# One 512-column product for the hi weights in the last feed-forward, with the second block's divided at changing columns

## The chip, the cores and the metric

The kernel runs on one core of one Trainium2 chip. The metric is the device time of one execution in microseconds. Times are compared by the median of several runs; one execution is also recorded by the hardware profiler, and all durations below come from that one.

## What is computed

One inference step of a small two-layer transformer backbone for two groups of 128 tokens each: 128 context tokens and 128 latent tokens, model width 2048. Both groups use the same weights, so the kernel treats them as one operand with 256 token columns (NT = 256). Each layer has an attention mixer and a gated feed-forward with a three-wide convolution over the tokens:

```python
def conv_ffn(h, w_up, w_conv, b_conv, w_down):
    u = h @ w_up                                  # 2048 -> 2 * 5632
    up = jnp.pad(u, ((0, 0), (1, 1), (0, 0)))
    u = up[:, :-2] * w_conv[0] + up[:, 1:-1] * w_conv[1] + up[:, 2:] * w_conv[2] + b_conv
    gate, val = u[..., :D_FF], u[..., D_FF:]
    return (jax.nn.silu(gate) * val) @ w_down     # 5632 -> 2048
...
    h = rmsnorm(x, g_norm_ffn[l]) * (1 + sc2) + sh2
    x = x + gt2 * conv_ffn(h, w_ffn_up[l], w_ffn_conv[l], b_ffn_conv[l], w_ffn_down[l])
```

The factors sh, sc and gt come from a modulation product of the conditioning vector with w_ada. All data are float32.

## The kernel before, in words

**Products in three parts.** Activations lie with features on the partitions and the 256 tokens in the columns. To multiply at TensorE's reduced-precision float32 rate, each float32 operand is split into a hi part (rounded) and a lo part (the rest). A product of weights and operand is then hi·hi + hi·lo + lo·hi; lo·lo is dropped. The function `split` makes the parts: ScalarE casts the hi part (L238) and VectorE subtracts it for the lo part (L239). An operand row `hx[:, k]` holds 512 columns, the 256 of hi and behind them the 256 of lo (ROW = 512); the intermediate rows `g` of the feed-forward are laid out in the same way.

**One product.** `gemm` computes one output chunk of 128 features. It runs over the blocks of 128 input features: 16 in an up product, 22 in a down product. For each block it issues three matmuls of 256 columns into the same columns of one PSUM bank (tile acc, three banks in rotation): wh by x-hi, wh by x-lo, wl by x-hi. All matmuls are recorded under one helper's line, L105.

**Weights.** `Weights.chunk` hands out the blocks of a product. SP loads 1 MB tiles (raw, three buffers); the hi and lo parts are made 8 blocks at a time in tiles wh and wl with four buffers each, so that up to two up products can be made ahead of TensorE.

**The feed-forward** (`ffn`, called once for each layer) is done in two halves of the 5632 inner features. In each half, `up` makes 22 gate and 22 value products. After each, `conv` does the convolution: ScalarE scales and adds the bias (L1275), and VectorE adds the two neighbours (L1278, L1281), all three reading PSUM. SiLU, the product of gate and value (L1298) and their split into `g` follow. Then `down` makes 16 products of 22 blocks, and `residual` adds each to x with the gate factor, one VectorE instruction per token group (L775). The first products of a feed-forward are special: three are begun ahead, four more have a written order, and in five (list WIDER) the first matmul takes some columns more (32, 16, 8, 4 and 2) into unused columns of the bank.

**What sets the order.** A scheduler with a simulated timeline orders each engine's instructions; only some are kept in the written order. Between products, `pump` inserts part of the remaining modulation work; in the last feed-forward this is a product of a 2048-wide row on VectorE (L454, 2.3 us), 24 of them in all, spread at a rate of 0.7 per product until they are used up.

Of the kernel before, what the change touches and what calls it, by code (L numbers as in the profile page):

```python
# [13 lines left out]
ALU = mybir.AluOpType  # L14
# [3 lines left out]
P = 128  # L18
D = 2048
KD = D // P  # L20
T = 128
NT = 2 * T
ROW = 2 * NT
SHIFT = 320
NL = 2
# [30 lines left out]

EARLY = (2, 5, 8, 11, 13)
WIDER = (32, 16, 8, 4, 2)
SENT = (1, 3, 6, 9, 12, 14, 16)
FINE = 4  # L60

# [28 lines left out]
def step_kernel(ctx: ExitStack, tc: tile.TileContext, A: dict):  # L90
    nc = tc.nc
    dve, act, pool, sp = nc.vector, nc.scalar, nc.gpsimd, nc.sync
    kept = []

    def keep_order(i):
        if not any(i is j for j in kept):
            kept[:] = [i]
            tc.keep_in_program_order(i)
# [16 lines left out]
    pe = TensorE()  # L115
# [3 lines left out]
    tmp = ctx.enter_context(tc.tile_pool(name="tmp", bufs=2))  # L119
    small = ctx.enter_context(tc.tile_pool(name="small", bufs=4))  # L120
    pacc = ctx.enter_context(tc.tile_pool(name="pacc", bufs=3, space=PSUM))
# [5 lines left out]
    def banks(name):  # L127
        return tc.tile_pool(name=name, bufs=1, space=PSUM)
# [3 lines left out]
    def nm(s):  # L132
        uid[0] += 1
        return f"{s}_{uid[0]}"

    def T_(pl, shape, tag, dt=F32, bufs=None):
        kw = {} if bufs is None else {"bufs": bufs}
        return pl.tile(shape, dt, tag=tag, name=nm(tag), **kw)
# [50 lines left out]
    def stat_add(st, src, n, eng=pool):  # L189

        st["n"] += 1
        if st["n"] == 1:
            st["acc"] = T_(keep, [P, NT], "sqacc")
            act.activation(st["acc"], src, AF.Square)
            return
        sq = T_(tmp, [P, NT], "sq", bufs=2)
        act.activation(sq, src, AF.Square)  # L197
        if st["n"] == n:
            st["last"] = sq
        else:  # L200
            eng.tensor_tensor(out=st["acc"], in0=st["acc"], in1=sq, op=ALU.add)  # L201
# [35 lines left out]
    def split(out_hi, out_lo, src, pin=lambda i: i):  # L237
        pin(act.copy(out_hi, src))  # L238
        pin(dve.tensor_tensor(out=out_lo, in0=src, in1=out_hi.bitcast(F32), op=ALU.subtract))  # L239
# [84 lines left out]
    def gemm(blocks, xh, xl, n=NT, first=0, between=None, more=None):  # L324

        fixed = lambda i: keep_order(i) if between is not None else i
        ps = T_(pacc, [P, 512], "acc")
        last = len(blocks) - 1  # L330
        for i in range(last + 1):
            k = (i + first) % (last + 1)
            wh, wl = blocks[k]
            x0 = more(k) if more and i == 0 else xh(k)
            fixed(pe.matmul(ps[:, :x0.shape[-1]], wh, x0, start=(i == 0), stop=False))
            if callable(between):
                if i == (last + 1) // 2:
                    between()
            elif between and i in between:
                between[i]()  # L340
            fixed(pe.matmul(ps[:, :n], wh, xl(k), start=False, stop=False))
            fixed(pe.matmul(ps[:, :n], wl, xh(k), start=False, stop=(i == last)))
        return ps[:, :n]

    ada = {"i": 2, "t": 0, "due": 0.0, "pew": 1.0}
    feat = {"i": 0, "t": 0, "due": 0.0}
# [316 lines left out]
    def raw_tile(pl, tag):  # L665
        return home(pl, tag)[:, :KD * 2 * UW].rearrange("p (k n) -> p k n", k=KD)
# [105 lines left out]
    def residual(ps, l, which, c, st=None):  # L772
        for g in range(2):
            s = slice(g * T, (g + 1) * T)
            dve.scalar_tensor_tensor(out=x[:, c, s], in0=ps[:, s],  # L775
                                     scalar=mod[:, l, 3 * which + 2, c, g:g + 1],
                                     in1=x[:, c, s], op0=ALU.mult, op1=ALU.add)
        if st is not None:
            stat_add(st, x[:, c], KD)
# [467 lines left out]

    def ffn(hx, W, ready, turn, l, st):
        xh, xl = (lambda k: hx[:, k, :NT]), (lambda k: hx[:, k, NT:2 * NT])
        wider = list(WIDER)  # L1250

        def product():
            if ready:
                return ready.pop(0)
            if in_order:
                return gemm(W.chunk(), xh, xl, between=in_order.pop(0))
            if wider:
                n = NT + wider.pop(0)
                return gemm(W.chunk(), xh, xl, more=lambda k: hx[:, k, :n])
            return gemm(W.chunk(), xh, xl)  # L1260

        WD = Weights(A["w_down"][l], KQ, TB)
        cw = ada["cw"]
        with tc.tile_pool(name=f"ffn{l}", bufs=1) as fp, banks(f"pffn{l}") as pf:
            feat["home"], feat["pool"] = fp, pf
            feat["due"] = 0.0
            in_order = [{}, {}] + turn + [{}]
            T_(fp, [P, SHIFT // 4], "pad")

            def conv(m):  # L1270
                early = bool(ready)
                pin = keep_order if early else lambda i: i
                ps = product()
                y = T_(fp, [P, NT], "cv", bufs=3)
                pin(act.activation(y, ps, AF.Identity, scale=cw[:, 1, m:m + 1], bias=cw[:, 3, m:m + 1]))  # L1275
                y3 = y.rearrange("p (g t) -> p g t", g=2)
                p3 = ps.rearrange("p (g t) -> p g t", g=2)
                pin(dve.scalar_tensor_tensor(out=y3[:, :, 1:], in0=p3[:, :, :T - 1],  # L1278
                                             scalar=cw[:, 0, m:m + 1], in1=y3[:, :, 1:],
                                             op0=ALU.mult, op1=ALU.add))  # L1280
                pin(dve.scalar_tensor_tensor(out=y3[:, :, :T - 1], in0=p3[:, :, 1:],  # L1281
                                             scalar=cw[:, 2, m:m + 1], in1=y3[:, :, :T - 1],
                                             op0=ALU.mult, op1=ALU.add))
                if early and ready:
                    W.ahead(pin)
                return y

            def up(q):
                gs = []
                for i in range(q * KQ, (q + 1) * KQ):  # L1290
                    rate = 0 if i < LATE else FRATE["up"]
                    fine[0] = False
                    gate = conv(i)
                    pump(0, rate)
                    val = conv(NFF + i)
                    pump(0, rate)
                    act.activation(gate, gate, AF.Silu)
                    dve.tensor_tensor(out=val, in0=gate, in1=val, op=ALU.mult)  # L1298
                    g = T_(fp, [P, ROW], "g", F32R, bufs=KQ)
                    split(g[:, :NT], g[:, NT:2 * NT], val)  # L1300
                    gs.append(g)
                    if i == LATE - 1:
                        load_row()
                return gs

            def down(gs, q):
                u, rows = None, None
                if q == NQ - 1 and l < NL - 1:
                    u = raw_tile(keep, "hx")
                    rows = raw_rows(u, l + 1, 0)  # L1310
                for c in range(KD):
                    quiet = q == NQ - 1 and c >= KD - QUIET[0]
                    fine[0] = quiet
                    if q == 0:
                        ensure(l, 5, [c // 4])
                    ps = gemm(WD.chunk(), lambda k: gs[k][:, :NT], lambda k: gs[k][:, NT:2 * NT])
                    if l == NL - 1 and q == NQ - 1 and c == KD - 1:
                        last_residual(ps, l, 1, c, st)
                    else:
                        residual(ps, l, 1, c, st if q == NQ - 1 else None)  # L1320
                    if rows:
                        rows(c)
                    if l == NL - 1 and q == NQ - 1 and c in EARLY:
                        act.activation(x[:, c], x[:, c], AF.Identity, scale=C("gfin")[:, c:c + 1])
                    pump(0, 0 if quiet else FRATE["down"])
                return u

            for q in range(NQ):
                gs = up(q)
                u = down(gs, q)  # L1330
            while feat["i"] < FLIMIT[stage[0]]:
                feature_step()
            return u


    with banks("pab") as ppool["ada"]:
# [10 lines left out]
        hx = operand(keep, "hx")  # L1347
        st = stat_init()
        with tc.tile_pool(name="beside", bufs=1) as beside:
            o = mixer_ab(hx, rb0, beside)  # L1350
            with tc.tile_pool(name="raw", bufs=1) as rp:
# [3 lines left out]
                W = Weights(A["w_up"][0], KD, 1)  # L1355
# [5 lines left out]
    with tc.tile_pool(name="cc", bufs=1) as cp, banks("pc") as ppool["ada"]:  # L1361
# [3 lines left out]
        W = Weights(A["w_in_c"], KD, 1)  # L1365
# [5 lines left out]
        W = Weights(A["w_up"][1], KD, 1)  # L1371
# [7 lines left out]
    for c in range(KD):  # L1379
# [5 lines left out]
        if c == 0:  # L1385
            act.copy(rbs, rb)
        if c + 1 in SENT:
            sp.dma_start(out=A["o_y"][:, sent:c + 1], in_=x[:, sent:c + 1])
# [132 lines left out]
```

## Time and profile before

| What | Value |
|---|---|
| median of 3 runs | 2337.18 us (2333.8 to 2337.86) |
| the profiled execution's own time | 2337.88 us |
| its span, first to last instruction | 2336.0 us |
| mean granted TensorE clock | 0.995 |
| moved by DMA, mean rate | 612.97 MB, 262 GB/s |
| end of the last product's matmuls | 2323 us of the span |

The page of the profile gives busy time by engine, the chain of work that ended last, and groups of instructions by source line. A row of a timeline has the start in us, the length in us, engine, line, operation, output and inputs, shapes and the count of merged instructions. A matmul's listed length overlaps the next one's, because matmuls are pipelined: what one costs is the distance from its start to the start of the next. A row of a table by stretches has the stretch, its length, and the busy time with the count of instructions for PE (matmul), PEld (weight load), DVE, ACT and POOL, then the granted clock, the DMA share and GB/s.

### The profile page before, as it was taken

Reading aid. Unit: us, or ns where it says so; the run is one execution under the profiler, and the core shown is the slowest. Engines: PE = TensorE matmul, PEld = TensorE weight load, DVE = VectorE, ACT = ScalarE, POOL = GpSimd, SP = SyncE. Lnnn points to the kernel's source line nnn. Section 1 sums busy time; section 2 is a strip of 40 time slices with the busy share of each in tenths; the row PEclk is TensorE's granted clock in tenths of the full one; section 3 lists DMA queues with packets and bytes.
Section 4 is the critical chain, followed back from the end, with each engine's and each line's share of the span. In section 5 each row is a group of like instructions: output and inputs, shape, how many; then the busy total and the mean of one; then the engine's idle time right before and its main releaser. Section 6 shows DMA issues by size and latency. Waiting matters only on the chain.

```text
span 2336.0 us, 47894 instructions
## 1 busy us (share of the span) xinstructions
PE 2298.1 (98%) x19666; PEld 2188.7 (94%) x19666; DVE 1850.7 (79%) x2864; ACT 1193.6 (51%) x1980; POOL 177.0 (8%) x242
## 2 busy tenths in 40 slices
PE   6999999999999999999999999999999999999998
PEld 5689778999999999999999999999999999999998
DVE  3569767889999999999988888798899755666654
ACT  4245555575553355555564444457655434555543
POOL 0002111210000000001130000023000000000011
PEclk9999999999999999999999999999999999999999
DMA  9988888677767777777778898777677555555553
GB/s 365 347 336 290 314 311 325 236 294 264 261 253 290 292 268 269 268 257 258 284 292 274 297 313 306 244 277 265 240 261 265 196 199 190 192 197 198 188 194 126
DMA packets 106811, 612.97 MB, mean 262 GB/s; under 512 B 11552, under 2 KB 19552, under 8 KB 38880
## 3 DMA queue, kind: packets, MB, share of 16 engines
q1 hardware_dynamic: 106592, 609.92, 71.6%
q8 instruction: 154, 2.52, 0.4%
q14 instruction: 65, 0.53, 0.1%
HBM read 605.12 MB, written 4.75 MB: 261 GB/s over the span
## 4 chain that ended last, share of the span: by engine, by line
PE 95%; DVE 2%; DMA 2%; ACT 1%; issue 0%; SPq 0%; POOL 0%; DVEq 0%; ACTq 0%
PE acc L105 86%; PE ada L105 4%; PE att L105 2%; DMA araw<-w_ada 1%; PE att L108 1%; DVE wl L239 1%; DMA block<-w_ada 1%; PE misc L105 1%; PE ada L108 0%; DVE aacc L483 0%; DMA raw<-w_in_ab 0%; ACT wh L238 0%; DVE x L1383 0%; DVE nt L606 0%; DVE ql L879 0%
## 5 line engine op out<-in xcount | busy, mean ns | idle before, releaser
L238 ACT CAST wh<-raw 128x1024 fp32r<-128x1024 f32 (+2 forms) x824 | 794.9, 976 | 934.1 <-PE acc L105 757.6
L105 PE MATMUL acc<-hx,wh 128*128 128x256 f32 (+1 forms) x7296 | 1263.9, 278 | 6.3 <-ACT hx L616 4.3
L239 DVE TENSOR_TENSOR wl<-raw,wh 128x1024 fp32r<-128x1024 f32 (+2 forms) x824 | 919.6, 1132 | 287.8 <-ACT wh L238 282.0
L105 PEld LDWEIGHTS acc<-hx,wh 128*128 128x128 f32 x7296 | 1104.8, 188 | 38.6 <-issue 15.5
L105 PE MATMUL acc<-hx,wl 128*128 128x256 f32 (+1 forms) x3648 | 1010.5, 277 | 4.5 <-DVE wl L239 4.5
L105 PEld LDWEIGHTS acc<-hx,wl 128*128 128x128 f32 x3648 | 686.8, 188 | 5.6 <-DVE wl L239 5.5
L105 PE MATMUL acc<-g,wh 128*128 128x256 f32 x2816 | 478.9, 276 | 0.0
L105 PEld LDWEIGHTS acc<-g,wh 128*128 128x128 f32 x2816 | 423.7, 188 | 0.0
L105 PE MATMUL acc<-g,wl 128*128 128x256 f32 x1408 | 388.2, 276 | 0.0
L105 PE MATMUL acc<-hxc,wh 128*128 128x256 f32 (+1 forms) x1536 | 276.4, 281 | 0.0
L454 DVE CUSTOM_DVE_ANT_0 junk<-araw,condb 128x2048 f32<-128x2048 f32 x120 | 275.8, 2298 | 0.0
L105 PEld LDWEIGHTS acc<-g,wl 128*128 128x128 f32 x1408 | 264.2, 188 | 0.0
L105 PEld LDWEIGHTS acc<-hxc,wh 128*128 128x128 f32 x1536 | 235.9, 188 | 8.7 <-issue 8.4
L105 PE MATMUL acc<-hxc,wl 128*128 128x256 f32 (+1 forms) x768 | 213.4, 278 | 0.0
L201 POOL TENSOR_TENSOR sqacc<-sqacc,sq 128x256 f32<-128x256 f32 x62 | 71.0, 1146 | 1514.3 <-ACT sq L197 1507.8
L483 DVE SCALAR_TENSOR_TENSOR aacc<-block,condw,aacc 128x512 f32<-128x512 f32 x240 | 172.0, 753 | 13.6 <-DMA block<-w_ada 13.4
L105 PEld LDWEIGHTS acc<-hxc,wl 128*128 128x128 f32 x768 | 144.4, 188 | 0.3
L105 PE MATMUL ada<-araw,condw 128*32 128x512 f32 (+1 forms) x736 | 91.3, 591 | 13.2 <-DMA araw<-w_ada 13.2
L1275 ACT ACTIVATE cv<-acc,convw 128x256 f32<-128x256 f32 x170 | 94.9, 558 | 0.0
L775 DVE SCALAR_TENSOR_TENSOR x<-acc,mod,x 128x128 f32<-128x128 f32 x190 | 57.4, 343 | 37.6 <-PE acc L105 37.5
L1281 DVE SCALAR_TENSOR_TENSOR cv<-acc,convw,cv 128x254 f32<-128x254 f32 x170 | 81.3, 479 | 3.3
L1278 DVE SCALAR_TENSOR_TENSOR cv<-acc,convw,cv 128x254 f32<-128x254 f32 x170 | 80.7, 475 | 0.0
(229 smaller groups left out, 1400.1 us busy)
## 6 DMA issues: line engine op xcount, KB each, us to landing
raw<-w_up SPq DMA_DIRECT2D x176, 1024.0 KB, 4.8
araw<-w_ada SPq DMA_DIRECT2D x146, 1024.0 KB, 6.1
raw<-w_down SPq DMA_DIRECT2D x88, 1024.0 KB, 4.8
raw<-w_in_c SPq DMA_DIRECT2D x48, 1024.0 KB, 6.8
block<-w_ada SPq DMA_DIRECT2D x128, 256.0 KB, 5.5
raw<-w_in_ab SPq DMA_DIRECT2D x19, 1024.0 KB, 7.4
raw<-w_out_ab SPq DMA_DIRECT2D x16, 1024.0 KB, 7.3
raw<-w_out_c SPq DMA_DIRECT2D x16, 1024.0 KB, 5.7
```

The lines of the kernel that those rows point to most:

```text
L105: return self.placed(nc.tensor.matmul(*a, **kw))
L108: return self.placed(nc.tensor.transpose(*a, **kw))
L201: eng.tensor_tensor(out=st["acc"], in0=st["acc"], in1=sq, op=ALU.add)
L238: pin(act.copy(out_hi, src))
L239: pin(dve.tensor_tensor(out=out_lo, in0=src, in1=out_hi.bitcast(F32), op=ALU.subtract))
L454: keep_order(dve.tensor_tensor_reduce(out=T_(feat["pool"], [P, D], "junk"), in1=feat["row"][:, c], in0=feat["raw"].rearrange("p g n -> p ( ...
L483: i = dve.scalar_tensor_tensor(out=acc[c], in0=block, scalar=condw[:, k, c:c + 1], in1=acc[c], op0=ALU.mult, op1=ALU.add)
L775: dve.scalar_tensor_tensor(out=x[:, c, s], in0=ps[:, s], scalar=mod[:, l, 3 * which + 2, c, g:g + 1], in1=x[:, c, s], op0=ALU.mult, op1=AL ...
L1275: pin(act.activation(y, ps, AF.Identity, scale=cw[:, 1, m:m + 1], bias=cw[:, 3, m:m + 1]))
L1278: pin(dve.scalar_tensor_tensor(out=y3[:, :, 1:], in0=p3[:, :, :T - 1], scalar=cw[:, 0, m:m + 1], in1=y3[:, :, 1:], op0=ALU.mult, op1=ALU.add))
L1281: pin(dve.scalar_tensor_tensor(out=y3[:, :, :T - 1], in0=p3[:, :, 1:], scalar=cw[:, 2, m:m + 1], in1=y3[:, :, :T - 1], op0=ALU.mult, op1=A ...
```

## The change

In the last layer's feed-forward only, a new function `wide_product` takes the place of `gemm`. For each block it issues one matmul of wh with the whole 512-column row, hi and lo side by side, and one matmul of wl with the 256 hi columns. A product thus fills a whole bank: columns 0 to 255 hold hi·hi + lo·hi, columns 256 to 511 hold hi·lo. The two halves are added afterwards. In an up product, VectorE copies the first half out of PSUM and adds the second; the convolution then reads the sum in SBUF. In a down product, `residual` is called twice, once with each half.

In the second block (k = 1) the 512-column matmul is divided in two at a column taken in turn from the list CUTS; where the entry is 0 it isn't divided. The special first products and the last two down products of the second half stay as they were.

```diff
+CUTS = (256, 384, 288, 320, 272, 264, 0)
...
+    def wide_product(blocks, xs, cut):
+
+        ps = T_(pacc, [P, 512], "acc")
+        last = len(blocks) - 1
+        for k, (wh, wl) in enumerate(blocks):
+            for a, b in ((0, cut), (cut, ROW)) if k == 1 and cut else ((0, ROW),):
+                pe.matmul(ps[:, a:b], wh, xs(k)[:, a:b], start=(k == 0), stop=False, skip_group_check=True)
+            pe.matmul(ps[:, :NT], wl, xs(k)[:, :NT], start=False, stop=(k == last), skip_group_check=True)
+        return ps
...
-        wider = list(WIDER)
+        wider, cuts = list(WIDER), list(CUTS)
...
-            return gemm(W.chunk(), xh, xl)
+            if l < NL - 1:
+                return gemm(W.chunk(), xh, xl)
+            cuts.append(cuts.pop(0))
+            ps = wide_product(W.chunk(), lambda k: hx[:, k], cuts[-1])
+            t = T_(tmp, [P, NT], "nt", bufs=4)
+            dve.tensor_copy(out=t, in_=ps[:, :NT])
+            dve.tensor_tensor(out=t, in0=t, in1=ps[:, NT:], op=ALU.add)
+            return t
...
-                    ps = gemm(WD.chunk(), lambda k: gs[k][:, :NT], lambda k: gs[k][:, NT:2 * NT])
+                    if l == NL - 1 and (q == 0 or c < KD - 2):
+                        cuts.append(cuts.pop(0))
+                        ps = wide_product(WD.chunk(), lambda k: gs[k], cuts[-1])
+                        residual(ps[:, NT:], l, 1, c)
+                        ps = ps[:, :NT]
+                    else:
+                        ps = gemm(WD.chunk(), lambda k: gs[k][:, :NT], lambda k: gs[k][:, NT:2 * NT])
```

## The prediction

> **What bounds the kernel now.** I read the page's busy line and its chain first, then a table by stretches of the last feed-forward, then TensorE's timeline inside that stretch.
>
> ```profile
> PE 2298.1 (98%) x19666; PEld 2188.7 (94%) x19666; DVE 1850.7 (79%) x2864; ACT 1193.6 (51%) x1980; POOL 177.0 (8%) x242
> PE 95%; DVE 2%; DMA 2%; ACT 1%; issue 0%; SPq 0%; POOL 0%; DVEq 0%; ACTq 0%
> PE acc L105 86%; PE ada L105 4%; PE att L105 2%; DMA araw<-w_ada 1%; PE att L108 1%; DVE wl L239 1%; DMA block<-w_ada 1%; PE misc L105 1%; PE ada L108 0%; DVE aacc L483 0%; DMA raw<-w_in_ab 0%; ACT wh L238 0%; DVE x L1383 0%; DVE nt L606 0%; DVE ql L879 0%
> ```
>
> TensorE is the bound: 95% of the chain is PE, and 86% are the matmuls into acc. There are as many weight loads as matmuls: each matmul brings its own load, also where two in a row use the same weights. Now the stretch that the change touches (columns: PE, PEld, DVE, ACT, POOL busy us and counts, clock, DMA).
>
> ```profile
> 1660.00:1790.00 130.00, 130.00 (x1149) 130.00 (x1149) 121.36 (x156) 69.33 (x97) 0.00 (x0) 1.00 0.74 268
> 1790.00:2300.00 510.00, 510.00 (x4503) 510.00 (x4502) 326.29 (x428) 248.32 (x319) 14.06 (x11) 1.00 0.56 196
> ```
>
> PE is without a gap over 640 us at a full granted clock, so here time is the number of matmuls times their spacing: 510 us / 4503 = 113.3 ns. Nothing but that spacing, or a wait that does not exist today, can move this stretch. The spacing is not the same everywhere, and that is the heart of the case (start us, us, form, count).
>
> ```profile
> 1526.04 0.40 PE L105 MATMUL acc<-hx,wh 128*128 128x256 f32 x2
> ...
> 1528.16 0.40 PE L105 MATMUL acc<-hx,wh 128*128 128x256 f32 x2
> ...
> 2000.07 0.39 PE L105 MATMUL acc<-hx,wh 128*128 128x256 f32 x2
> ...
> 2003.81 0.39 PE L105 MATMUL acc<-hx,wh 128*128 128x256 f32 x2
> ```
>
> From 2000.07 to 2003.81 eleven blocks of three matmuls pass: 3.74 us / 33 = 113.3 ns, a "close rhythm". From 1526.04 to 1528.16, in the layer's output projection, six blocks of the same three 256-column matmuls take 2.12 us: 117.8 ns each, a "loose rhythm", with no wait and the same clock. Each rhythm keeps itself up for many matmuls. The stretch of the change lies wholly in the close one: a block (hi·hi, hi·lo, lo·hi) costs 340.0 ns.
>
> **The change part by part.** In the changed program's order, 76 products of 16 blocks (up) and 30 of 22 (down) become wide: 1876 blocks. TensorE's instructions fall by 1785 (18987 to 17202): 1876 joined pairs, of which 91 are cut in two again. Everything ahead of the first wide product is the same on every engine.
>
> *The joined matmul.* A block becomes one of 512 columns and one of 256. No 512-column matmul of this kind is in the trace. Nearest are the 384-column ones, and the single widened matmuls that open some products:
>
> ```profile
> 229.94 0.51 PE L105 MATMUL acc<-kv_in,wh 128*128 128x384 f32 x2
> ...
> 231.50 0.51 PE L105 MATMUL acc<-kv_in,wh 128*128 128x384 f32 x2
> ...
> 308.65 0.52 PE L105 MATMUL acc<-kv_in,wh 128*128 128x384 f32 x2
> ...
> 310.24 0.51 PE L105 MATMUL acc<-kv_in,wh 128*128 128x384 f32 x2
> ...
> 496.45 0.41 PE L105 MATMUL acc<-hx,wh 128*128 128x288 f32 x2
> ...
> 496.82 0.41 PE L105 MATMUL acc<-hx,wh 128*128 128x256 f32 x2
> ...
> 497.18 0.39 PE L105 MATMUL acc<-hx,wh 128*128 128x256 f32 x2
> ...
> 497.52 0.39 PE L105 MATMUL acc<-hx,wh 128*128 128x256 f32 x2
> ...
> 1653.90 0.40 PE L105 MATMUL acc<-hx,wh 128*128 128x264 f32 x2
> ...
> 1654.26 0.39 PE L105 MATMUL acc<-hx,wh 128*128 128x256 f32 x2
> ```
>
> Nine matmuls of 384 columns take 1.56 us (173.3 ns each) in one place and 1.59 us (176.7) in another: two rhythms again. Bounds for 512 columns. From below: a block that opens with 264 columns takes 0.36 us and one with 288 takes 0.37, 0.01 us for 24 columns or 0.42 ns a column; 256 more columns on a 113.3 ns matmul give 220.8 ns. From above: from 113.3 (256) to 173.3 (384) a column costs 0.469 ns; carried on to 512 that is 233.3. Between them lies 2 x 113.3 = 226.7 ns, at which joining saves nothing, and the line from the loose 256 (117.8) through 173.3, which gives 228.8. I take 227.5, on the 384 side, since those matmuls are wide all the time, as the new ones are, while the 288 is a single one in a train of 256s.
>
> *The 256 after it.* After the 288 the two next blocks take 0.36 and 0.34 us: a wide one breaks the close rhythm, and it needs a block or so to come back. In a wide product a wide one comes in every block, so I expect the lo·hi matmul between 113.3 and 117.8 and take 115.5, the middle. Block: 227.5 + 115.5 = 343 ns, 3 ns more than now: 1876 x 3 = +5.6 us. Ends: 220.8 + 113.3 = 334.1 (-11.1 us) and 233.3 + 117.8 = 351.1 (+20.8).
>
> *The cuts.* In 91 second blocks the 512 columns go as 256+256 (16 times) or as a wide and a narrow one (384+128, 288+224, 320+192, 272+240, 264+248, 15 times each). A narrow one brings a weight load of its own, and loads follow each other at 113 ns here, so I price it 113 whatever its width. The wide parts at 0.469 ns a column: 173, 128, 143, 121, 117. Against 227.5 that is about +59, +14, +29, +7 and +3, and 0 for the halves: 15 x 112 = +1.7 us. Lower end 0. The upper end is that a narrow one runs as slowly as plain fp32, which the trace has (two records for each matmul):
>
> ```profile
> L105 PE MATMUL att<-pT,vm 128*128 128x128 f32 x48 | 7.5, 285 | 0.2 <-ACT pT L816 0.2
> L105 PE MATMUL att<-dv,pT 128*128 128x256 f32 x48 | 11.7, 378 | 0.0
> ```
>
> 24 matmuls (8 heads by 3) in 7.5 and in 11.7 us are 0.31 us at 128 and 0.49 at 256 columns, against 0.113: some 0.28 us more for each of the 75 narrow ones, +21 us. All other reduced-precision matmuls here have 256 columns or more, so no row excludes it.
>
> *VectorE.* Each wide up product adds a copy out of PSUM and an addition; each wide down product adds a second residual of two instructions.
>
> ```profile
> L833 DVE TENSOR_SCALAR p<-p,rec 128x256 f32<-128x256 f32 x16 | 5.6, 350 | 0.0
> L750 DVE TENSOR_TENSOR nt<-acc,sq 128x256 f32<-128x256 f32 x9 | 3.7, 413 | 0.1
> L775 DVE SCALAR_TENSOR_TENSOR x<-acc,mod,x 128x128 f32<-128x128 f32 x190 | 57.4, 343 | 37.6 <-PE acc L105 37.5
> L454 DVE CUSTOM_DVE_ANT_0 junk<-araw,condb 128x2048 f32<-128x2048 f32 x120 | 275.8, 2298 | 0.0
> ```
>
> The copy is like L833 (0.35 us), the addition like L750 (0.41): +0.76 us per up product of 5.44 us. Down: 2 x 0.343 = 0.69 us in 7.5 us. From 1790 on VectorE is busy 326 of 510 us, so all of this lies beside the matmuls; without that cover it would be 76 x 0.76 + 30 x 0.69 = 78 us. From 1660 to 1790 it is busy 121.4 of 130 us, because the modulation rows of 2.3 us (L454) still run there. In the changed order the 22 of them behind the first wide product are spread over 33 products instead of 30. Then: 30.5 products at 93% are 155 us; 2.5 more without rows, at 3.6 us each, 9; 33 x 0.76 = 25; together 189 us for 33 x 5.44 = 180 us of PE. The 9 us must come out of VectorE's lead: four lo-weight buffers of 8 blocks are two products, 10.9 us. What is queued behind the new copy, which waits for its product's last matmul, is the next lo-weights, and TensorE waits for these only when the lead is used up. Bounds 0 and 9 us; I take +1.
>
> *The rest.* ScalarE's and VectorE's convolution steps read the copy instead of PSUM: same counts. A PSUM bank is held by copy and addition instead of three reads: no wait, three banks rotate. The DMAs and their sizes are the same; in SP's order only the loads of modulation rows slip behind some of the weights', and nothing on TensorE waits for those rows. The last two products and the end are unchanged.
>
> Sum: +5.6 + 1.7 + 1.0 = +8.3 us on the profiled execution's 2337.9 us (span 2336.0), which stands 0.7 us above the median of 2337.2: **2345 us**.
>
> **The rivals.**
>
> *The close rhythm holds for the joined pair (ends faster).* Block 334.1 ns: -11.1 us, +1.7 for the cuts, and 0 to 4 us for VectorE, whose cover shrinks: 2328 to 2332. For it: the extra columns of 264 to 288 cost only 0.42 ns each; a 256 train falls back into 113.3 soon after a disturbance; the cuts change the phase in each product, so that a bad one need not last. Against it: not one 384 train is as close (113.3 + 128 x 0.42 would be 167 ns; 173.3 and 176.7 are seen). It decides from a block below 339 ns.
>
> *The weight load sets the spacing.* If 113.3 ns is the load's and not the matmul's, taking away one load of three saves more: 512 x 0.42 = 215 ns and 113.3 make 328 ns, -22 us, of which VectorE takes some 5 back: about 2321. Against it: if the load were the limit, a few columns more would be free, and 264 columns already lengthen the block.
>
> *Joining saves next to nothing.* A block of 338 to 341 ns, cuts +1.7, VectorE 0 to 3: 2334 to 2341. The Trainium skill, "TensorE: Matmul & The Clock Gate", section Back-to-back issue gap, gives columns / 2.4 plus 2.5 ns; by it a block would fall from 327.5 to 325.0 ns and the sum be -4.7 + 1.7 + 1.0 = -2.0 us. The trace does not agree for 256 columns: 113.3 ns against its 109.2; for 512 no run so far shows it.
>
> *Narrow pieces at plain fp32 rate.* +21 instead of +1.7: 2357 to 2366. *VectorE becomes the bound* for the first 33 products: +9 instead of +1: 2350 to 2355.
>
> That the change does not do what it says is excluded by the order of its instructions.
>
> **How the numbers follow.** Forecast, 2342 to 2350: 0.40. Close rhythm: 0.32. Load sets the pace: 0.05. Next to nothing: 0.14. Narrow pieces: 0.05. VectorE: 0.04. Faster and slower count from 0.2% (4.7 us), about what a measurement can tell: faster 0.32 + 0.05 = 0.37; same 0.14; slower 0.40 + 0.05 + 0.04 = 0.49. As both signs hold much, the forecast's own range is 2342 to 2350; the range that leaves out no more than 2 in 10 reaches from 2326 (most of the close-rhythm case) to 2353 (the forecast and part of the VectorE case).
>
> **What would show it.** In the changed profile, right: blocks in the timeline 0.343 us apart from about 1670 to 2308, wide ones starting 0.227 before the lo·hi one; narrow pieces at about 0.11; no PE wait for wl L239. Wrong: blocks at 0.334 (close rhythm) or 0.328 (load); pieces of 0.3 us and more; PE idle with VectorE as its releaser before 1850; or a spacing that differs from product to product, so that a mean hides several rhythms.

## The result, and the profile after

The changed kernel takes 2366.1 us (median of 4 runs, 2363.1 to 2369.0) against 2337.5 us, a ratio of 1.0120 with a 95% interval of 1.0108 to 1.0133: 28.6 us slower, where 2345 us had been forecast with a range up to 2353. The sign was right, the size was not: +8.3 us had been summed up.

First the page of the changed kernel: the busy line, then the chain. Lines of the source have moved by one to 24; the matmul helper is L106 now.

```profile
PE 2322.7 (98%) x17881; PEld 2130.8 (90%) x17881; DVE 1921.3 (81%) x3076; ACT 1198.9 (51%) x1980; POOL 177.0 (7%) x242
PE 94%; DMA 2%; DVE 2%; ACT 1%; issue 0%; SPq 0%; POOL 0%; DVEq 0%; ACTq 0%
```

TensorE does 1785 matmuls fewer and is busy 24.6 us longer. It is still what ends the kernel. The table by stretches of the same 640 us shows why nothing else is to blame:

```profile
1660.00:1790.00 130.00, 130.00 (x782) 115.11 (x781) 122.83 (x182) 65.33 (x88) 0.00 (x0) 1.00 0.70 247
1790.00:2300.00 510.00, 509.12 (x2948) 445.75 (x2947) 379.25 (x585) 244.63 (x308) 10.59 (x8) 1.00 0.55 191
```

The clock is granted in full, and VectorE, busy 379 us of the second stretch instead of 326, stays below TensorE. PE idles for 0.9 of 640 us, in one wait for VectorE's residual (L786):

```profile
PE acc L106 <- DVE x L786: 0.9, 1, 0.9
```

So nearly all of the time sits in the spacing of the matmuls. A row of matmuls that follow each other without a wait is called a train below. In the timeline of the changed kernel the last 258-column matmul, the first joined one at 1668.21, the first block with a cut at 384 and the end of the last down product read as follows:

```profile
1662.75 0.40 PE L106 MATMUL acc<-hx,wh 128*128 128x258 f32 x2
...
1668.10 0.28 PE L106 MATMUL acc<-hx,wl 128*128 128x256 f32 x1
1668.21 0.39 PE L106 MATMUL acc<-hx,wh 128*128 128x512 f32 x1
1668.43 0.28 PE L106 MATMUL acc<-hx,wl 128*128 128x256 f32 x1
1668.55 0.40 PE L106 MATMUL acc<-hx,wh 128*128 128x256 f32 x2
1668.79 0.28 PE L106 MATMUL acc<-hx,wl 128*128 128x256 f32 x1
1668.91 0.40 PE L106 MATMUL acc<-hx,wh 128*128 128x512 f32 x1
...
1672.44 0.40 PE L106 MATMUL acc<-hx,wh 128*128 128x512 f32 x1
1672.67 0.28 PE L106 MATMUL acc<-hx,wl 128*128 128x256 f32 x1
...
1674.21 0.40 PE L106 MATMUL acc<-hx,wh 128*128 128x384 f32 x2
1674.44 0.33 PE L106 MATMUL acc<-hx,wl 128*128 128x256 f32 x1
1674.61 0.39 PE L106 MATMUL acc<-hx,wh 128*128 128x512 f32 x1
...
2348.32 0.28 PE L106 MATMUL acc<-g,wl 128*128 128x256 f32 x1
```

The first joined matmul takes 0.22 us (1668.21 to 1668.43), twice 113 ns. After that the close rhythm is gone: from 1668.91 to 1672.44 ten blocks take 3.53 us, 353 ns each instead of 340: a joined matmul 0.235, the lo·hi one 0.118. The kernel before has the same two marks, the first and the last row here (the row between them is used further down).

```profile
1664.81 0.28 PE L105 MATMUL acc<-hx,wh 128*128 128x258 f32 x1
...
1665.17 0.40 PE L105 MATMUL acc<-hx,wh 128*128 128x256 f32 x2
...
2322.96 0.28 PE L105 MATMUL acc<-g,wl 128*128 128x256 f32 x1
```

From mark to mark it is 685.6 us after and 658.2 before: +27.4 us. (The two profiled executions differ by 25.2 us as a whole; the changed one reached the first mark 2.1 us sooner.) Of the 27.4, 1876 blocks by 13.3 ns are 25.0 us, and 0.9 is the wait for VectorE. The blocks with a cut add 1.4 us, of which the blocks behind them give some 0.5 back. The last two down products add 0.6: they run in the loose rhythm too, though nothing in them was changed.

### The profile page after: what moved, and what is told of

Same layout as the page of the kernel before. It is cut to its first block, busy times and chain, and to the rows that moved or that the text cites. A ratio compares the mean times of both kernels' runs of the same rounds, so it can differ in the third digit from the quotient of the medians.

```text
span 2360.9 us, 44404 instructions
## 1 busy us (share of the span) xinstructions
PE 2322.7 (98%) x17881; PEld 2130.8 (90%) x17881; DVE 1921.3 (81%) x3076; ACT 1198.9 (51%) x1980; POOL 177.0 (7%) x242
## 4 chain that ended last, share of the span: by engine, by line
PE 94%; DMA 2%; DVE 2%; ACT 1%; issue 0%; SPq 0%; POOL 0%; DVEq 0%; ACTq 0%
PE acc L106 86%; PE ada L106 4%; PE att L106 2%; DMA araw<-w_ada 1%; PE att L109 1%; DVE wl L240 1%; DMA raw<-w_in_ab 1%; PE misc L106 1%; DMA block<-w_ada 0%; PE ada L109 0%; ACT wh L239 0%; DVE aacc L494 0%; DVE x L1407 0%; DVE nt L617 0%; DVE ql L890 0%
## 5 line engine op out<-in xcount | busy, mean ns | idle before, releaser
L106 PE MATMUL acc<-hx,wh 128*128 128x256 f32 (+2 forms) x6145 | 1278.2, 301 | 5.4 <-ACT hx L627 4.1
L106 PEld LDWEIGHTS acc<-hx,wh 128*128 128x128 f32 x6145 | 973.3, 188 | 90.7 <-issue 15.3
L106 PE MATMUL acc<-hx,wl 128*128 128x256 f32 (+1 forms) x3648 | 1016.5, 279 | 4.5 <-DVE wl L240 4.5
L106 PEld LDWEIGHTS acc<-hx,wl 128*128 128x128 f32 x3648 | 686.1, 188 | 5.8 <-DVE wl L240 5.7
L106 PE MATMUL acc<-g,wh 128*128 128x256 f32 (+1 forms) x2182 | 488.3, 312 | 0.9 <-DVE x L786 0.9
L106 PE MATMUL acc<-g,wl 128*128 128x256 f32 x1408 | 391.7, 279 | 0.0
L106 PEld LDWEIGHTS acc<-g,wh 128*128 128x128 f32 x2182 | 352.5, 188 | 30.3 <-PE acc L106 1.2
L106 PE MATMUL acc<-hxc,wh 128*128 128x256 f32 (+1 forms) x1536 | 276.6, 281 | 0.0
L106 PEld LDWEIGHTS acc<-g,wl 128*128 128x128 f32 x1408 | 264.3, 188 | 0.3
L106 PEld LDWEIGHTS acc<-hxc,wh 128*128 128x128 f32 x1536 | 236.0, 188 | 8.7 <-issue 8.4
L106 PE MATMUL acc<-hxc,wl 128*128 128x256 f32 (+1 forms) x768 | 213.5, 278 | 0.0
L106 PEld LDWEIGHTS acc<-hxc,wl 128*128 128x128 f32 x768 | 144.5, 188 | 0.3
L786 DVE SCALAR_TENSOR_TENSOR x<-acc,mod,x 128x128 f32<-128x128 f32 x250 | 73.5, 342 | 39.0 <-PE acc L106 38.9
L106 PE MATMUL ada<-araw,condw 128*32 128x512 f32 (+1 forms) x736 | 91.1, 590 | 13.8 <-DMA araw<-w_ada 13.8
L106 PEld LDWEIGHTS ada<-araw,condw 128*32 128x32 f32 x736 | 18.6, 111 | 39.4 <-issue 16.1
L1293 ACT ACTIVATE cv<-acc,convw 128x256 f32<-128x256 f32 x94 | 52.5, 559 | 0.0
L1293 ACT ACTIVATE cv<-nt,convw 128x256 f32<-128x256 f32 x82 | 49.2, 600 | 4.1 <-DVE g L240 2.6
```

Of the source, the lines that this page charges most:

```text
L106: return self.placed(nc.tensor.matmul(*a, **kw))
L786: dve.scalar_tensor_tensor(out=x[:, c, s], in0=ps[:, s], scalar=mod[:, l, 3 * which + 2, c, g:g + 1], in1=x[:, c, s], op0=ALU.mult, op1=AL ...
```

## The experiments

Theory A, which the runs test: what a matmul costs here is its columns times one of two paces, 0.443 ns a column in the close rhythm (113.3 / 256) and 0.460 in the loose one (117.8 / 256). There is no fixed part per instruction that joining could save, and the joined matmul throws the train into the loose pace. Rivals: B, the cuts do it; C, VectorE's added evacuation or the bank's second half does it; D, the addresses of weights and operand do it.

In the expectations, "phase" means how the matmuls of a train lie in time to each other.

**No cuts (e1_nocut).**

```diff
-CUTS = (256, 384, 288, 320, 272, 264, 0)
+CUTS = (0,)
```

> The changed kernel with no second block divided (the 512-column product stays whole in all 1876 blocks). Theory A, paces by column: a matmul here costs its columns at one of two paces, 0.443 or 0.460 ns a column, the joined pair brings no gain even at the close pace (227 + 113 = 340 ns a block), and the alternation of 512 and 256 columns lapses into the loose one by itself: blocks stay at 353 ns, time 2363 to 2368 us. Rival B, the cuts: each division shifts the phase and throws the product out of the close pace; without them blocks come at 340 ns and the time is 2338 to 2343 us. Rival C, the evacuation (VectorE's copy and addition, the second half of the bank): 353 ns as in A.

Measured: 2367.4 us, ratio 1.0135 (1.0118 to 1.0152). Its table by stretches:

```profile
1660.00:1790.00 130.00, 130.00 (x775) 114.47 (x774) 122.84 (x180) 65.40 (x88) 0.00 (x0) 1.00 0.69 245
1790.00:2300.00 510.00, 507.81 (x2865) 440.59 (x2864) 378.96 (x585) 243.19 (x306) 9.20 (x7) 1.00 0.57 192
```

2865 matmuls in 507.8 us are 177 ns each, half of a block of 354. B falls: without any division the pace is as loose. The cuts neither cause the loss nor, in the change, lead out of it.

**All divided at 256 (e2_all256, e2b_all256).** Three matmuls of 256 columns again, everything else of the change kept.

```diff
-            for a, b in ((0, cut), (cut, ROW)) if k == 1 and cut else ((0, ROW),):
-                pe.matmul(ps[:, a:b], wh, xs(k)[:, a:b], start=(k == 0), stop=False, skip_group_check=True)
+            for a, b in ((0, NT), (NT, ROW)):
+                pe.matmul(ps[:, a:b], wh, xs(k)[:, a:b], start=(k == 0 and a == 0), stop=False, skip_group_check=True)
```

In e2_all256 `start` is as in the change, on both halves of the first block, and the first block's hi·hi is missing from the product; e2b_all256 is as printed.

> The changed kernel with every 512-column product divided at 256: three matmuls of 256 columns a block as before the change, but hi.lo still goes to the second half of the bank, and VectorE's copy, addition and second residual stay. Theory A: an even train of 256s holds the close pace, 340 ns a block, 2337 to 2342 us. Rival C, the evacuation or the bank's second half makes the loose pace: 353 ns a block, 2362 us or more. Rival B says nothing here but that no phase is shifted: as A.

> The changed kernel with every 512-column product divided at 256, the first half's first matmul alone clearing the bank. Three matmuls a block, VectorE's copy, addition and second residual stay. Theory A: close pace, 340 ns a block, no difference from the kernel before, 2336 to 2341 us. Rival C, the evacuation: 2350 us or more.

Measured: e2_all256 2339.4 us, ratio 1.0008 (0.9998 to 1.0019), and e2b_all256 2336.5 us, ratio 0.9991 (0.9982 to 1.0001). The table of e2b_all256:

```profile
1660.00:1790.00 130.00, 130.00 (x1150) 130.00 (x1149) 126.53 (x186) 68.07 (x92) 0.00 (x0) 1.00 0.71 259
1790.00:2300.00 510.00, 510.00 (x4503) 510.00 (x4502) 390.83 (x607) 256.25 (x325) 13.62 (x11) 1.00 0.56 199
```

4503 matmuls in 510 us, the very count of the kernel before, with VectorE at 391 us instead of 326 and at 126.5 of 130 in the first stretch. C falls: copy, addition and second residual lie wholly beside the matmuls here, and writing to the bank's second half costs nothing. What costs is the joining.

**The pace alone (e5_nowider).** The kernel before, without the widened first matmuls.

```diff
-WIDER = (32, 16, 8, 4, 2)
+WIDER = ()
```

> The kernel before without the five widened first matmuls of each feed-forward, all else the same. It weighs the pace alone, with no join and no added VectorE work. Theory A: before the widened ones the last feed-forward ran at 117.8 ns a matmul and would stay there, some 5900 matmuls by 4.45 ns = +26 us, 2360 to 2366 us; the first feed-forward was close already and stays. If the pace were an effect of load or evacuation and not of the train's phase: 2338 us, no difference.

Measured: 2363.2 us, ratio 1.0118 (1.0103 to 1.0133): within 3 us as slow as the change, with no joined matmul and no added work. Its second stretch:

```profile
1790.00:2300.00 510.00, 510.00 (x4333) 510.00 (x4332) 317.53 (x414) 237.55 (x306) 10.65 (x8) 1.00 0.54 190
```

510 us / 4333 = 117.7 ns: the same train, in the loose rhythm from end to end. It entered the stretch loose, and nothing led it out. Ahead of the stretch, the kernel before shows a train that turns loose and comes back:

```profile
1633.51 0.39 PE L105 MATMUL acc<-hx,wh 128*128 128x256 f32 x2
...
1633.85 0.28 PE L105 MATMUL acc<-hx,wh 128*128 128x256 f32 x1
1633.97 0.60 PE L108 MATMUL misc<-cst,am 128*128 128x128 f32 x4
...
1634.65 0.40 PE L105 MATMUL acc<-hx,wh 128*128 128x256 f32 x2
...
1642.77 0.41 PE L105 MATMUL acc<-hx,wh 128*128 128x288 f32 x2
...
1643.14 0.40 PE L105 MATMUL acc<-hx,wh 128*128 128x256 f32 x2
...
1648.44 0.41 PE L105 MATMUL acc<-hx,wh 128*128 128x272 f32 x2
...
1649.14 0.39 PE L105 MATMUL acc<-hx,wh 128*128 128x256 f32 x2
```

Up to 1633.85 a block takes 0.34 us. Then plain float32 matmuls of 128 columns come between (L108, the modulation work), and from 1634.65 to 1642.77 23 blocks take 8.12 us, 353 ns each. The 288-column matmul at 1642.77 changes nothing: 15 blocks from 1643.14 to 1648.44 take 5.30 us, 353 ns again. The 272-column one at 1648.44 leads back: from 1649.14 to the row at 1653.90 that the prediction shows, 14 blocks take 4.76 us, 340 ns each. So a train turns loose behind other things than a 512-column matmul too, and of two widened ones it was the narrower that helped.

**The addresses (e4_offsets).** Without cuts, and with four more floats in each weight buffer, which puts each 32 bytes further from the one before (4128 bytes instead of 4096).

```diff
-                        wh_ = T_(wpool, [P, 1024], "wh", F32R, bufs=4)
-                        wl_ = T_(wpool, [P, 1024], "wl", F32R, bufs=4)
+                        wh_ = T_(wpool, [P, 1028], "wh", F32R, bufs=4)
+                        wl_ = T_(wpool, [P, 1028], "wl", F32R, bufs=4)
```

(The two lines in `halves` likewise, and CUTS as in e1_nocut.)

> The changed kernel without divisions, and each of the four hi and four lo weight buffers lies 32 bytes further than the one before, so that the weights start at 64, 96, 0 and 32 bytes past a multiple of 128 in turn. Rival D, the addresses: the pace depends on how weights and operand lie to each other; blocks of some buffers come at 340 ns or below and others at 353 or above, in a pattern of four half products. Theory A, phase of the train alone: 353 ns in all, about 2365 us.

One run: 2408.1 us. Its table shows the first feed-forward, whose code is that of the kernel before, and the last one:

```profile
530.00:1150.00 620.00, 620.00 (x5268) 620.00 (x5267) 556.85 (x706) 297.55 (x401) 9.02 (x6) 1.00 0.73 259
1675.00:2300.00 625.00, 622.71 (x3653) 549.74 (x3652) 501.31 (x761) 310.23 (x398) 2.85 (x2) 1.00 0.60 205
```

The kernel before does 5473 matmuls in the first of these stretches; here it is 5268, 117.7 ns on average. That this is the loose rhythm's figure is chance, for the mean hides several rhythms. Each of these rows but the last opens 8 blocks from the next weight buffer:

```profile
708.74 0.40 PE L106 MATMUL acc<-hx,wh 128*128 128x256 f32 x2
...
711.48 0.40 PE L106 MATMUL acc<-hx,wh 128*128 128x256 f32 x2
...
714.31 0.39 PE L106 MATMUL acc<-g,wh 128*128 128x256 f32 x2
...
717.14 0.40 PE L106 MATMUL acc<-g,wh 128*128 128x256 f32 x2
...
720.05 0.40 PE L106 MATMUL acc<-g,wh 128*128 128x256 f32 x2
```

With weights that start at 64 bytes past a multiple of 128, as all do in the kernel before, 8 blocks take 2.74 us; at 96, 0 and 32 bytes they take 2.83, 2.83 and 2.91. Over the first feed-forward the median block takes 340 ns at 64, and 354, 352 and 356 at 96, 0 and 32, where single blocks reach 388. This is the pattern of four half products that rival D foresaw, in plain trains. So the pace depends on addresses too, and a train is not bound to two rhythms; a train that comes from a slow buffer is close again one block into the good one (from 709.10 on a block takes 0.34 us). Joined blocks in the last feed-forward have medians of 350 to 353 ns at all four offsets, so no offset tried brings them near 340. The change itself moves no weight buffer, so D does not explain its loss.

**Longer matmuls throughout (e3_uni512).** Here lo·lo is added as well, and there are no cuts (CUTS as in e1_nocut).

```diff
-            pe.matmul(ps[:, :NT], wl, xs(k)[:, :NT], start=False, stop=(k == last), skip_group_check=True)
+            pe.matmul(ps, wl, xs(k), start=False, stop=(k == last), skip_group_check=True)
```

> The changed kernel without divisions, and the lo weights also meet the whole row: two 512-column matmuls a block, an even train of long ones (it adds lo.lo, which the others leave out, so it has a third more columns and its time is read by the block alone). Theory A1, it is the alternation of 512 and 256 that loses the close pace: an even train keeps it, 2 x 226.7 = 453 ns a block, about 2338 + 1876 x 0.113 = 2550 us. Theory A2, the length itself: 2 x 235.5 = 471 ns a block, about 2584 us. A fixed part for each instruction, as the prediction's first rival has it, would show as a column price of 0.42 ns: 2 x 221 = 442.

One run: 2580.0 us. In its timeline,

```profile
2000.06 0.39 PE L106 MATMUL acc<-g,wh 128*128 128x512 f32 x1
2000.29 0.40 PE L106 MATMUL acc<-g,wl 128*128 128x512 f32 x1
...
2003.79 0.39 PE L106 MATMUL acc<-g,wh 128*128 128x512 f32 x1
```

sixteen matmuls take 3.73 us: 233 ns each, 0.455 ns a column. An even train of long ones doesn't hold the close pace either; A1 falls, A2 is met within 4 us. But 0.455 is neither of theory A's two paces: the hi matmuls take 0.231 us and the lo ones 0.236. The price per column stays far above 0.42, so no fixed part per instruction shows.

**One joined block in four (e6_fourth).**

```diff
-            for a, b in ((0, cut), (cut, ROW)) if k == 1 and cut else ((0, ROW),):
+            for a, b in ((0, ROW),) if k % 4 == 0 else ((0, NT), (NT, ROW)):
```

> The changed kernel, but only each fourth block is joined and never divided; the others have three matmuls of 256 (copy and addition stay). A train of 256s that is disturbed by one 512 in twelve. Theory A1: if a 512 only disturbs while it comes in every block, the train falls back to 113.3 and the stretch costs little, about 2340 us; if one 512 is enough to throw the train into the loose pace and nothing in it leads back, all blocks take 353 ns, about 2364 us. In between the mean tells how long the way back is. Theory A2 gives 4.4 ns more for each 256 columns of the joined ones alone: about 2345 us.

One run: 2362.9 us. A quarter of the joined matmuls costs nearly the whole loss. That is the second case of A1's sentence: nothing leads the train back for long. The next two runs take it to the end.

**A single joined matmul, and the way back (e7_one, e8_one_back).** The kernel before, in which one block of one product is joined; e8_one_back repeats the five widened first matmuls behind it. The edits are against the changed kernel; the line with `wider.extend` is in e8_one_back alone.

```diff
-            for a, b in ((0, cut), (cut, ROW)) if k == 1 and cut else ((0, ROW),):
+            for a, b in ((0, ROW),) if k == 0 else ((0, NT), (NT, ROW)):
...
-            if l < NL - 1:
+            if l < NL - 1 or len(cuts) < len(CUTS):
                 return gemm(W.chunk(), xh, xl)
-            cuts.append(cuts.pop(0))
-            ps = wide_product(W.chunk(), lambda k: hx[:, k], cuts[-1])
+            cuts.pop(0)
+            wider.extend(WIDER)
+            ps = wide_product(W.chunk(), lambda k: hx[:, k], 0)
...
-                    if l == NL - 1 and (q == 0 or c < KD - 2):
+                    if False:
```

> The kernel before with one single joined matmul: in the last feed-forward's first plain up product the first block's two hi matmuls are one of 512 columns (that product alone has copy and addition); all other 1875 blocks are as before. Theory A1': the first joined matmul throws the train into the loose pace and nothing leads back, so almost the whole loss comes of one instruction: 353 ns a block, 2360 to 2365 us. Rival: each joined matmul pays for itself, by its 8.7 ns: no difference, 2336 to 2341 us.

> As e7_one, and the five products after that one get a widened first matmul again (288, 272, 264, 260 and 258 columns). Theory A1': one of the five leads back to the close pace, as the 272 did at the start of this stretch before the change; the loss is then at most 5 products by 0.2 us: 2336 to 2342 us. If the loose pace came of what the joined matmul leaves behind and not of the phase, the widened ones change nothing: 2360 to 2365 us.

Measured: e7_one 2362.7 us, ratio 1.0099 (1.0078 to 1.0121); e8_one_back 2337.3 us, ratio 0.9996 (0.9986 to 1.0006). First e7_one, from the one joined matmul on, and its second stretch:

```profile
1670.17 0.28 PE L106 MATMUL acc<-hx,wl 128*128 128x256 f32 x1
1670.28 0.39 PE L106 MATMUL acc<-hx,wh 128*128 128x512 f32 x1
1670.51 0.28 PE L106 MATMUL acc<-hx,wl 128*128 128x256 f32 x1
1670.63 0.40 PE L106 MATMUL acc<-hx,wh 128*128 128x256 f32 x2
...
1672.39 0.40 PE L106 MATMUL acc<-hx,wh 128*128 128x256 f32 x2
```

```profile
1790.00:2300.00 510.00, 510.00 (x4332) 510.00 (x4332) 317.62 (x414) 237.43 (x306) 10.65 (x8) 1.00 0.54 190
```

Five blocks of plain 256s take 1.76 us (1670.63 to 1672.39), 352 ns each, and from 120 us later on it is still 117.7 ns a matmul. The joined matmul itself takes 0.23 us, no more than two close ones; what costs 24 us is the rhythm that it leaves behind. Then e8_one_back around the 288-column matmul:

```profile
1673.16 0.40 PE L106 MATMUL acc<-hx,wh 128*128 128x256 f32 x2
...
1673.51 0.42 PE L106 MATMUL acc<-hx,wh 128*128 128x288 f32 x2
...
1673.88 0.40 PE L106 MATMUL acc<-hx,wh 128*128 128x256 f32 x2
...
1674.23 0.39 PE L106 MATMUL acc<-hx,wh 128*128 128x256 f32 x2
...
1674.57 0.39 PE L106 MATMUL acc<-hx,wh 128*128 128x256 f32 x2
```

Blocks of 0.35 us before it, 0.37 and 0.35 with it, 0.34 from 1674.23 on. The widened matmul, 32 columns of needless work, buys back 24 us. Here the 288 led back at once, where in the kernel before the 288 did not and the 272 did: which width helps depends on how the train lies, and no run shows a rule for it.

**Other company (e9_ratios).** Could any neighbour give the joined matmul the close pace? The lo matmul gets another width in each product (the columns over 256 add part of lo·lo).

```diff
-CUTS = (256, 384, 288, 320, 272, 264, 0)
+CUTS = (256, 260, 264, 272, 288, 320, 384, 448)
...
-            for a, b in ((0, cut), (cut, ROW)) if k == 1 and cut else ((0, ROW),):
+            for a, b in ((0, ROW),):
...
-            pe.matmul(ps[:, :NT], wl, xs(k)[:, :NT], start=False, stop=(k == last), skip_group_check=True)
+            pe.matmul(ps[:, :cut], wl, xs(k)[:, :cut], start=False, stop=(k == last), skip_group_check=True)
```

> The changed kernel without divisions, and in each product the lo weights' matmul takes another width in all its blocks: 256, 260, 264, 272, 288, 320, 384, 448 columns in turn (the columns over 256 add part of lo.lo, which the others leave out; read by the spacing, not by the time). Does any company give the 512-column matmul the close pace? If the loose pace is a matter of the pair's rhythm, some widths show 226.7 ns for the 512 and 0.443 ns a column in all; if a matmul of 512 columns cannot hold the close pace, all widths stay above 0.455 ns a column, as the even train of 512s did (466.7 ns for 1024).

One run, 2406.7 us with its extra columns. Read by block, the eight widths gave 0.459, 0.458, 0.460, 0.462, 0.463, 0.449, 0.454 and 0.454 ns a column. That is neither of the outcomes written down: none reaches 0.443, and three lie below 0.455. With 320 columns:

```profile
1700.22 0.39 PE L106 MATMUL acc<-hx,wh 128*128 128x512 f32 x1
1700.44 0.31 PE L106 MATMUL acc<-hx,wl 128*128 128x320 f32 x1
...
1700.96 0.39 PE L106 MATMUL acc<-hx,wh 128*128 128x512 f32 x1
...
1701.71 0.39 PE L106 MATMUL acc<-hx,wh 128*128 128x512 f32 x1
```

Four blocks in 1.49 us, 373 ns: the 512 takes 0.22 us, as two close 256s, and the 320 stays loose. So a 512-column matmul can run at the close pace beside some neighbours, and the pace is not a matter of its length alone. But at its best a joined matmul costs what the two it replaces cost, and no version here beats the kernel before.

## Why the prediction was wrong

- *The bound: right.* TensorE's spacing set this stretch, and still does, but for one wait of 0.9 us.
- *The step that failed: the block at 343 ns.* Both of its terms were taken between two rhythms, where the changed train has one of them. The prediction had written that each rhythm keeps itself up for many matmuls and did not draw the conclusion: once thrown out, with nothing leading back, the whole stretch is loose. The block measures 353.3 ns, so this step stood at +5.6 us and came to +25.0.
  - *The joined matmul*, "I take 227.5", takes 235 ns in nearly every block: 14 us of the miss. That is the loose pace times the columns, 0.460 x 512 = 235.5, and two rows of the prediction said so: 176.7 / 384 is 0.460, just as 117.8 / 256 is. The upper end, 233.3, was drawn from a close 256 to a 384 and so mixed the rhythms as well.
  - *The 256 after it*, "take 115.5, the middle", takes 118: 5 us of the miss. That "it needs a block or so to come back" was read from a widened matmul in a close train; e7_one shows that behind a 512 it does not come back.
- *The range.* The block's upper end, 351.1, was nearly met, but the range of the time left it out.
- *The cuts: right.* +1.7 us was forecast; the blocks with a cut took 1.4 us more than the others. The block at 1674.21 takes 0.40 us instead of 0.35: the 384 and the 128 together last 0.23, as a whole 512 does, but the lo·hi matmul behind them lasts 0.17 (1674.44 to 1674.61) instead of 0.12. Over all blocks with a cut at 384, 320, 288, 272 and 264 it is +49, +22, +11, +5 and +6 ns, where +59, +29, +14, +7 and +3 had been priced. With the wide piece and a loose 256 taken off, a narrow piece costs 107 to 121 ns whatever its width, near the 113 of the prediction. That its weight load is the reason was the prediction's argument; no run separates it. The plain fp32 rate is excluded.
- *VectorE: right in size, by another wait.* The copy took 0.42 us and the addition 0.42 instead of 0.35 and 0.41. The +1 was priced for the lo-weights; what came was the 0.9 us behind the residual (L786), 1.9 us in e1_nocut and none in e2b_all256, though VectorE is busy 97% of its first stretch.
- *The last two products: not unchanged.* They stand in the same train and are loose too: +0.6 us.
- *The rivals.* "Close rhythm holds" was given 0.32 and took 0.42 ns a column from two widened blocks of 0.36 and 0.37 us. That was no price per column: in the kernel before, a block that opens with 258 columns takes 0.36 us as well (1664.81 to 1665.17). Two more columns cost as much as eight, so what these rows measure is the disturbance. "Load sets the pace" is excluded: a third of the loads went and nothing got faster. The Trainium skill ("Perfetto Trace Analysis", section Matmuls) advises larger matmuls where possible, as more efficient than smaller ones. These runs do not agree: one of 512 took 226 ns at best and mostly 235, two close ones of 256 take 226.7. The Trainium skill's gap formula ("TensorE: Matmul & The Clock Gate", section Back-to-back issue gap), cited in the prediction, gives 215.8 ns for 512 columns, less than these runs show.

That the forecast had the right sign is partly luck: its +8.3 us came from a mean that no block showed.

What stays open is why there are such rhythms. The paces depend on the order of lengths and on addresses; they do not need VectorE's added load, the cuts or a smaller number of weight loads. "Columns times one of two paces" fits the feed-forward of the kernel before, the uncut blocks of the change and the runs with one joined matmul; the first 384-column row (0.451 ns a column), e3_uni512, e4_offsets and e9_ratios show paces between and beyond. What inside TensorE makes them was not separated.

## What to carry to other kernels

Before pricing a longer or a shorter matmul, divide spacings by columns: if two lengths give the same quotient, a cost per instruction that could be saved doesn't show. Where one train shows two spacings, ask which one the changed train will be in and what would lead it back, and forecast one or the other, not the mean; a single odd matmul can decide over hundreds of microseconds behind it. A cheap irregularity put once at the start is worth trying against a train that runs slow at a full clock without waits; several widths have to be tried, since here one did nothing and the next led back. And look one instruction further before calling a piece cheap: the price of the narrow pieces stood in the spacing of the matmul behind them.

## What the runs showed of the hardware that was not expected

With the buffers where the kernel before has them, a train of 256-column matmuls of this kind has two self-sustaining spacings, 113.3 and 117.7 ns, at the same granted clock and with no wait. One 512-column matmul moved it from the first to the second (e7_one, +24 us), and behind short plain float32 matmuls put between it was in the second as well (kernel before, 1633.97). One 288-column matmul moved it back in e8_one_back; in the kernel before a 288 did not and a 272 did.

The start of the weights matters: in e4_offsets 8 blocks of plain 256s took 2.74 us with weights 64 bytes past a multiple of 128, and 2.83, 2.83 and 2.91 us at 96, 0 and 32 bytes.

A 512-column matmul cut into 384 and 128 lasts no longer by the starts, 0.23 us, but the next matmul then lasts 0.17 us instead of 0.12.
